# Transposes of a hybrid decoder layer on TensorE, issued in pairs of groups

## Chip, core and metric

One core of one Trainium2 chip runs the whole kernel. The metric is the device time of one execution in microseconds (us), the median of several executions of the same program.

## What is computed

The kernel is one layer of a decoder trunk on 512 tokens of width 1024, in float32. Three mixers share one input projection, each output is gated, projected, and merged:

```python
h = rmsnorm(x, g_pre[i])
(gq, gk, gv, ga, gz, dq, dk, dv, iq, ik, iw, dz, xq, xz, gates) = split_cols(h @ w_in[i])
y_gla = gla_mixer(gq, gk, gv, ga, gz, w_gla_a_up[i], b_gla_a[i], g_gla[i])   # chunked linear attention, 4 heads
y_dsa = dsa_mixer(dq, dk, dv, iq, ik, iw, dz, rel_bias)                      # top-k attention, 8 heads, 2 kv heads
y_mem = cross_mixer(xq, xz, rmsnorm(mem, g_mem[i]), w_mem_kv[i])             # 256 memory tokens, 4 heads
s_gla, s_dsa, s_mem = jnp.split(jax.nn.sigmoid(gates), N_BRANCH, axis=-1)
merged = (s_gla * (y_gla @ w_gla_out[i]) + s_dsa * (y_dsa @ w_dsa_out[i]) + s_mem * (y_mem @ w_x_out[i]))
x = x + rmsnorm(merged @ w_o[i], g_post[i])
```

Each mixer ends in a product that contracts over keys or chunks, so its probabilities (or its normalised output) have to be transposed first. TensorE does that, 128x128 at a time, against an identity matrix.

## The kernel before

Every float32 product is made of three faster ones: each operand is split into a high part (ScalarE, `high`, L94) and the rest (VectorE, `low`, L98 and L100), and `mm3` (L107 to L109) adds high by high, high by low and low by high in one PSUM bank. The weights come in 1 MB loads on SyncE's queue and are split the same way (`whi`, `wlo`).

The program is a list of units, one per 128 columns of a weight matrix and 512 tokens. A unit has four quarters, and a quarter is six matmuls of 512 columns on TensorE (`unit_t`), or as many of 256 columns (`unit_n`). The order of the rest is written out by hand: `at(name, s, fn)` puts a piece of work behind quarter `s` of a unit (counted on into the following units), and the loop at the end of `trunk` (L1104) emits quarter by quarter what stands there. Pieces with the same slot are emitted in the order in which they were put. The engines then run their own queues in that order and meet by semaphores.

The pieces that matter here:

- `dsa_schedule` (L757) orders one pair of query heads, `hp` 0 to 3. A pair has eight pieces `c`: four blocks of 128 queries, `qb = c // 2`, times two heads. For each `c`, `dsa_bias` (GpSimd) adds position bias and mask, `dsa_probs` makes logits and exponentials, `dsa_norm` divides by the sum (VectorE), `dsa_turn` (L710) transposes the `qb + 1` blocks of probabilities into a PSUM bank `tpp` and takes the high part `pth` (ScalarE), `dsa_low` (L726) takes the low part `ptl` (VectorE), and once per two pieces `dsa_out` (L739) multiplies with the values into the PSUM bank `pov`; its second matmul (L108) is the first to read `ptl`. `step` is the distance between two pieces in quarters: 3 for `hp` 0, 2 for the others.
- `gla_y` (L650) transposes half of a linear attention head's output into a bank `to` (four transposes, L654), multiplies it with gain and gate on VectorE (L657) and splits it. `gla_turn_k` (L593) transposes keys into a bank `tk` (L597), with `kkl` as its low part. `gla_att` ends in the copy `attz` (L587) on VectorE.
- `x_turn` (L877) transposes the probabilities of 256 queries of a memory head into `xtp` (four transposes, L886) and splits them into `xpth` and `xptl`; `x_out` (L891) multiplies with the values into `xpo`.

`tpp`, `to`, `tk` and `xtp` take turns in the two PSUM buffers of the tag `tp` (`PSB`, L70): a bank is free again when both ScalarE and VectorE have read it.

Of the kernel before, what the change touches and what calls it, by code (L numbers as in the profile page):

```python
# [57 lines left out]
def trunk(ctx, tc, x, x_t, mem, w_in, w_c, w_kv, w_out, w_o, cols, g_mem, g_post, w_up, toe, out):  # L58
# [115 lines left out]
    def at(name, s, fn, *a):  # L174
        slots.setdefault(4 * where[name] + s, []).append((fn, a))
# [581 lines left out]
    def dsa_schedule(hp, name, step):  # L757
        def put(s, fn, *a):
            at(name, s, fn, hp, *a)
        put(-3, dsa_start)  # L760
        for c in range(8):
            put(4 + step * c, dsa_norm, c)
        for c in range(8):
            s = 2 + step * c
            put(max(s - 2, 1), dsa_bias, c)
            put(s, dsa_probs, c)
            put(s + 5, dsa_turn, c)
            put(s + 7, dsa_low, c)
            if c % 2:
                put(s + 9, dsa_out, c // 2)  # L770

    win_t("dk", dk_done)
# [222 lines left out]
    for h in range(4):  # L995
        z = f"gz{h}"
        if h < 2:
            at(z + ".0", h, gla_att, h, 0)
            at(z + ".0", h + 1, gla_att, h, 1)
            at(z + ".0", h + 2, gla_turn_k, h)  # L1000
            for p in range(3):
                at(z + ".1", 2*p + h, gla_state, h, p)
            after = 6 + h
        else:
            v = f"gv{h}"
            at(v + ".1", 0, gla_att, h, 0)
            at(v + ".1", 1, gla_att, h, 1)
            at(v + ".1", 2, gla_turn_k, h)
            for p in range(3):
                at(z + ".0", 2+p, gla_state, h, p)  # L1010
            after = 2
        for i in range(2):
            at(z + ".1", after + 2 * i, gla_out, h, i)
            at(z + ".1", after + 2 * i + 1, gla_norm, h, i)
            at(z + ".1", after + 10 + 2 * i, gla_y, h, i)
    for i in range(16):
        at("gz1.0", 2 + 6 * i, topk_max)
        at("gz1.0", 5 + 6 * i, topk_drop)
    at("gz1.0", 2 + 6 * 16, topk_mask)
    dsa_schedule(0, "gate02.0", 3)  # L1020
    for i in range(2):
        at("dq1.0", i, dsa_end, 0, i)
    for hp in range(1, 4):
        dsa_schedule(hp, f"dz{hp}.1", 2)
        for i in range(2):
            at(f"dz{hp}.1", 26 + i, dsa_end, hp, i)
# [5 lines left out]
    for h in range(4):  # L1032
        n = f"mv{h}.0"
        for i in range(2):
            for j in range(2):
                at(n, 1 + 4 * i + 2 * j, x_logits, h, i, j)
        at(n, 5, x_norm, h, 0)
        at(n, 9, x_norm, h, 1)
        at(n, 9, x_turn, h, 0)
        at(n, 11, x_turn, h, 1)  # L1040
        at(n, 13 if h == 0 else 17, x_out, h, 0)
        at(n, 15 if h == 0 else 19, x_out, h, 1)
# [8 lines left out]
    with tc.manual_schedule():  # L1051
# [7 lines left out]
        for k in range(4):  # L1059
            h, c = k // 2, slice(512 * (k % 2), 512 * (k % 2) + 512)  # L1060
# [114 lines left out]
def build(arrays):  # L1175
    import concourse.bacc as bacc
    nc = bacc.Bacc("TRN2", target_bir_lowering=False, num_devices=1, dynamic_dma_scratch_size=1024)
    aps = [nc.dram_tensor(n, v.shape, mybir.dt.from_np(v.dtype), kind="ExternalInput").ap()
           for n, v in arrays.items()]
    out = nc.dram_tensor("out", (T, D), F32, kind="ExternalOutput").ap()  # L1180
    with tile.TileContext(nc) as tc:
        trunk(tc, *aps, out)
    return nc
# [8 lines left out]
```

## Time and profile before

| | us |
|---|---|
| median of 3 runs | 834.88 (834.76 to 835.01) |
| the profiled execution, its own time | 834.8 |
| its span, first to last instruction | 833.1 |
| TensorE busy within the span | 818.7 |
| VectorE busy | 473.6 |
| ScalarE busy | 337.6 |
| GpSimd busy | 50.4 |

The sums below are made against the profiled execution, 834.8 us, of which 1.7 us lie outside the span; it stands 0.08 us under the median. In the views, PE is TensorE's matmul and PEld its weight load, DVE is VectorE, ACT is ScalarE, POOL is GpSimd. Matmuls are pipelined: the time that one takes of the stream is read from start to start, not from its duration.

### The profile page before, as it was taken

The numbers are of one execution on the slowest core, as the hardware profiler recorded it, in microseconds if no ns is written. First come the engines' busy times: TensorE is split into PE (matmuls) and PEld (weight loads), VectorE is DVE, ScalarE is ACT, GpSimd is POOL, SyncE is SP. The second block draws the span as 40 slices with busy tenths as digits, with TensorE's granted clock in tenths as the row PEclk, the third lists the DMA queues.
The fourth block names the chain that finished last, engine by engine and source line by source line (L and its number), as shares of the span: only waits on it lengthen the run. The fifth ranks groups of instructions, "written<-read, shape, count | busy, mean of one in ns | idle before, by whom it ended". The sixth has DMA issues, their size and how long they took to land.

```text
span 833.1 us, 10783 instructions
## 1 busy us (share of the span) xinstructions
PE 818.7 (98%) x4320; PEld 703.9 (84%) x4320; DVE 473.6 (57%) x850; ACT 337.6 (41%) x608; POOL 50.4 (6%) x74
## 2 busy tenths in 40 slices
PE   8989999999999999999999999999999999999997
PEld 7988888989888888888888888889989898888885
DVE  4759677888686435446676543545655554343623
ACT  6587554453423223334444422334434343322320
POOL 1000010010000030032131000000000000000000
PEclk9999999999999999999999999999999999999999
DMA  9324121121222231232131124322324142226402
GB/s 327 122 102 138 51 96 57 52 101 55 98 101 101 101 109 69 101 108 95 51 112 66 51 101 176 101 101 101 114 90 148 55 152 72 83 98 225 154 1 102
DMA packets 16387, 86.30 MB, mean 104 GB/s; under 512 B 2064, under 2 KB 2576, under 8 KB 7760
## 3 DMA queue, kind: packets, MB, share of 16 engines
q1 hardware_dynamic: 15472, 84.29, 28.4%
q10 hardware_dynamic: 864, 1.32, 0.4%
q8 instruction: 34, 0.56, 0.3%
q14 instruction: 17, 0.14, 0.0%
HBM read 82.42 MB, written 2.10 MB: 101 GB/s over the span
## 4 chain that ended last, share of the span: by engine, by line
PE 86%; ACT 5%; DVE 5%; DMA 3%; issue 2%; SPq 0%; DVEq 0%; POOLq 0%; POOL 0%; ACTq 0%
PE out L109 5%; PE out L108 5%; PE out L107 5%; PE pfin L109 2%; PE pfin L108 2%; PE pfin L107 2%; DMA wraw<-w_in 1%; DMA x<-x 1%; DVE wlo L98 1%; ACT whi L94 1%; PE tpp L721 1%; PE pov L108 1%; PE pov L109 1%; PE lg L108 1%; PE lg L109 1%
## 5 line engine op out<-in xcount | busy, mean ns | idle before, releaser
L98 DVE TENSOR_TENSOR wlo<-wraw,whi 128x1024 fp32r<-128x1024 f32 (+1 forms) x135 | 163.4, 1211 | 84.3 <-ACT whi L94 83.5
L94 ACT ACTIVATE whi<-wraw 128x1024 fp32r<-128x1024 f32 (+1 forms) x135 | 139.3, 1039 | 22.5 <-PE out L108 19.6
L107 PE MATMUL out<-yh,whi 128*128 128x512 f32 x192 | 75.3, 392 | 0.0
L109 PE MATMUL out<-yh,wlo 128*128 128x512 f32 x192 | 74.8, 390 | 0.0
L108 PE MATMUL out<-yl,whi 128*128 128x512 f32 x192 | 74.8, 389 | 0.0
L707 ACT ACTIVATE bm<-bm,nm 128x128 f32<-128x128 f32 (+3 forms) x32 | 18.0, 564 | 73.6 <-DVE nm L705 71.8
L691 POOL TENSOR_TENSOR bm<-toe,madd 128x128 f32<-128x128 f32 (+3 forms) x32 | 31.2, 993 | 194.4 <-DVE wlo L98 134.3
L109 PEld LDWEIGHTS out<-yh,wlo 128*128 128x128 f32 x192 | 36.0, 188 | 7.5
L107 PEld LDWEIGHTS out<-yh,whi 128*128 128x128 f32 x192 | 36.1, 188 | 7.3
L108 PEld LDWEIGHTS out<-yl,whi 128*128 128x128 f32 x192 | 36.1, 188 | 7.2
L94 ACT ACTIVATE yh<-th 128x512 fp32r<-128x512 f32 x16 | 10.1, 632 | 44.0 <-DVE th L657 24.9
L512 DVE SCALAR_TENSOR_TENSOR gth<-gth,out 128x512 f32<-128x512 f32 x16 | 11.0, 687 | 28.0 <-PE out L109 28.0
L273 POOL TENSOR_TENSOR rstd<-var,mhalf 128x1 f32<-128x1 f32 x6 | 3.3, 552 | 374.9 <-DVE var L952 289.7
L470 DVE MATCH_REPLACE8 madd<-m,madd 128x256 f32<-128x256 f32 (+2 forms) x48 | 25.6, 543 | 0.0
L466 DVE MAX8 m<-madd 128x8 f32<-128x256 f32 (+2 forms) x48 | 23.6, 547 | 0.0
L705 DVE CUSTOM_DVE_ANT_0 bm<-lg,bm 128x128 f32<-128x128 f32 (+3 forms) x32 | 15.5, 485 | 13.0 <-PE lg L109 7.6
L751 DVE TENSOR_TENSOR ydsa<-pov,th 128x128 f32<-128x128 f32 x32 | 7.8, 286 | 22.5 <-PE pov L109 22.1
L94 ACT ACTIVATE pth<-tpp 128x128 fp32r<-128x128 f32 (+3 forms) x32 | 13.7, 429 | 13.4 <-PE tpp L721 13.4
L456 DVE SCALAR_TENSOR_TENSOR madd<-relu,iw,madd 128x256 f32<-128x256 f32 (+2 forms) x21 | 12.9, 616 | 9.2 <-ACT relu L452 8.9
L949 ACT ACTIVATE sq<-pfin 128x512 f32<-128x512 f32 x8 | 4.8, 598 | 31.6 <-PE pfin L109 31.6
L98 DVE TENSOR_TENSOR yl<-th,yh 128x512 fp32r<-128x512 f32 x16 | 11.1, 692 | 11.2 <-ACT yh L94 11.2
L98 DVE TENSOR_TENSOR ptl<-tpp,pth 128x128 fp32r<-128x128 f32 (+3 forms) x32 | 15.4, 482 | 0.0
(1024 smaller groups left out, 2357.0 us busy)
## 6 DMA issues: line engine op xcount, KB each, us to landing
wraw<-w_in SPq DMA_DIRECT2D x43, 1024.0 KB, 4.8
wraw<-w_out SPq DMA_DIRECT2D x12, 1024.0 KB, 4.8
wraw<-w_kv SPq DMA_DIRECT2D x8, 1024.0 KB, 4.7
wraw<-w_o SPq DMA_DIRECT2D x4, 1024.0 KB, 4.8
x<-x SPq DMA_DIRECT2D x4, 512.0 KB, 9.1
toe<-toe SPq DMA_DIRECT2D x8, 256.0 KB, 5.2
xres<-x SPq DMA_DIRECT2D x4, 512.0 KB, 8.5
xt<-x_t SPq DMA_DIRECT2D x3, 512.0 KB, 7.8
```

Source lines behind the costliest of these rows:

```text
L94: act.activation(hi, src, AF.Copy, scale=scale)
L98: dve.tensor_tensor(lo, src, f(hi), op=OP.subtract)
L107: pe.matmul(o, lh, rh, start=first, stop=False)
L108: pe.matmul(o, lh, rl, start=False, stop=False)
L109: pe.matmul(o, ll, rh, start=False, stop=last)
L456: dve.scalar_tensor_tensor(sc, r[:, :n], iw[:, b, h:h + 1], sc, op0=OP.mult, op1=OP.add)
L466: dve.max(out=M8[b], in_=maskadd[b])
L470: dve.match_replace(out=maskadd[b], in_to_replace=M8[b], in_values=maskadd[b], imm_value=-FMAX)
L512: dve.scalar_tensor_tensor(th, th, 1.0, p, op0=OP.add, op1=OP.mult)
L691: pool.tensor_tensor(bm[:, :n], Q[hp]["toe"][i][:, 384 - 128 * qb:512], maskadd[qb], op=OP.add)
L705: dve.tensor_tensor_reduce(out=bm[:, :n], in0=lg[:, :n], in1=bm[:, :n], scale=-1.0, scalar=FMAX, op0=OP.add, op1=OP.min, accum_out=nm)
L707: act.activation(bm[:, :n], bm[:, :n], AF.Exp, scale=-1.0, bias=nm, accum_out=su)
```

## The change

Transposes that stood one group per head or half are put side by side: both pieces of one block of queries (`c - 1` and `c`) in the slot of the second, both halves of `gla_y` in one slot, both halves of `x_turn` in one slot. The low parts `dsa_low` of both pieces stand together too. Nothing is added or left out, and the slots of `dsa_out`, of the norms and of `x_out` stay.

```diff
             put(max(s - 2, 1), dsa_bias, c)
             put(s, dsa_probs, c)
-            put(s + 5, dsa_turn, c)
-            put(s + 7, dsa_low, c)
             if c % 2:
+                for d in (c - 1, c):
+                    put(s + 5, dsa_turn, d)
+                for d in (c - 1, c):
+                    put(s + 7, dsa_low, d)
                 put(s + 9, dsa_out, c // 2)
...
             at(z + ".1", after + 2 * i + 1, gla_norm, h, i)
-            at(z + ".1", after + 10 + 2 * i, gla_y, h, i)
+            at(z + ".1", after + 12, gla_y, h, i)
...
         at(n, 9, x_norm, h, 1)
-        at(n, 9, x_turn, h, 0)
+        at(n, 11, x_turn, h, 0)
         at(n, 11, x_turn, h, 1)
```

TensorE's queue in the last head pair (`hp` 3), around the `dsa_out` of its first block of queries (`pov`, which reads the pieces `c` 0 and 1), a piece of the difference; the other blocks of `hp` 1 to 3 read alike:

```order
-L721 MATMUL tpp<-ident,bm 128x128 x2
...
 L107 MATMUL pov<-pth,dvh 128x256
 L108 MATMUL pov<-ptl,dvh 128x256
 L109 MATMUL pov<-pth,dvl 128x256
-L721 MATMUL tpp<-ident,bm 128x128 x2
...
+L721 MATMUL tpp<-ident,bm 128x128 x4
```

Before, the transposes of the next even piece (`c` 2) stood ahead of `pov` and those of the odd piece (`c` 3) right behind it; now all four stand behind it, so `pov` comes earlier in TensorE's order by the transposes of the even piece.

VectorE's queue in head pair 2, second block of queries (`c` 2 and 3), before:

```order
L751 TENSOR_TENSOR ydsa<-pov,th 128x128 x2
L98 TENSOR_TENSOR ptl<-tpp,pth 128x2x128
L98 TENSOR_TENSOR wlo<-wraw,whi 128x1024
L736 RECIPROCAL rc<-su 128x1
L737 TENSOR_SCALAR bm<-bm,rc 128x384
L705 ISA bm,nm<-lg,bm 128x512
L705 ISA nm 128x1
L490 SCALAR_TENSOR_TENSOR th<-th,dz3.0_4001 128x512
L98 TENSOR_TENSOR ptl<-tpp,pth 128x2x128
```

and now:

```order
L751 TENSOR_TENSOR ydsa<-pov,th 128x128 x2
L98 TENSOR_TENSOR wlo<-wraw,whi 128x1024
L736 RECIPROCAL rc<-su 128x1
L737 TENSOR_SCALAR bm<-bm,rc 128x384
L705 ISA bm,nm<-lg,bm 128x512
L705 ISA nm 128x1
L490 SCALAR_TENSOR_TENSOR th<-th,dz3.0_3995 128x512
L98 TENSOR_TENSOR ptl<-tpp,pth 128x2x128 x2
```

The even piece's low part moved from ahead of the weight split `wlo` to directly ahead of the odd piece's, behind the gate `th` (L490).

VectorE's queue at the linear attention head 1, whose `gla_y` stands beside the keys' transposes of head 2 (a piece of the difference):

```order
-L657 SCALAR_TENSOR_TENSOR th<-to,col,th 128x512
-L98 TENSOR_TENSOR yl_1720<-th,yh_1719 128x512
 L587 COPY_PREDICATED attz<-cmask,pa 128x512
 L98 TENSOR_TENSOR al<-attz,ah 128x512
...
 L98 TENSOR_TENSOR kkl<-tk,kkh 128x384
 L98 TENSOR_TENSOR vl<-gv2.1_1672,vh 128x512
+L657 SCALAR_TENSOR_TENSOR th<-to,col,th 128x512
+L98 TENSOR_TENSOR yl_1764<-th,yh_1763 128x512
 L657 SCALAR_TENSOR_TENSOR th<-to,col,th 128x512
 L98 TENSOR_TENSOR yl_1774<-th,yh_1773 128x512
```

The first half's two instructions went from ahead of `attz` to behind `kkl`; on TensorE both `to` groups now follow `tk`, so the second one takes the bank that `tk` holds until `kkl` has read it.

## Rows read from the trace of the kernel before

**Rows 1.** The page: busy time of TensorE, and shares of the chain that ended last.
```profile
PE 818.7 (98%) x4320; PEld 703.9 (84%) x4320; DVE 473.6 (57%) x850; ACT 337.6 (41%) x608; POOL 50.4 (6%) x74
...
PE 86%; ACT 5%; DVE 5%; DMA 3%; issue 2%; SPq 0%; DVEq 0%; POOLq 0%; POOL 0%; ACTq 0%
```

**Rows 2.** Timeline of TensorE: start us, duration us, engine, line, operation. Eight transposes; four.
```profile
532.11 0.39 PE L109 MATMUL out<-yh,wlo 128*128 128x512 f32 x1
532.34 1.03 PE L294 MATMUL xps<-ident,xn 128*128 128x128 f32 x8
533.13 0.48 PE L107 MATMUL out<-yh,whi 128*128 128x512 f32 x1
533.44 0.40 PE L108 MATMUL out<-yl,whi 128*128 128x512 f32 x1
...
575.51 0.39 PE L109 MATMUL xq1.0_5296<-hh,wlo 128*128 128x512 f32 x1
...
576.41 0.40 PE L108 MATMUL xq1.0_5296<-hl,whi 128*128 128x512 f32 x1
```

**Rows 3.** Timeline: odd piece's low part, then the load of its reader; hp 1 to 3.
```profile
404.86 0.55 DVE L98 TENSOR_TENSOR ptl<-tpp,pth 128x384 fp32r<-128x384 f32 x1
406.22 0.19 PEld L108 LDWEIGHTS pov<-ptl,dvh 128*128 128x128 f32 x1
...
429.37 0.42 DVE L98 TENSOR_TENSOR ptl<-tpp,pth 128x256 fp32r<-128x256 f32 x1
430.23 0.19 PEld L108 LDWEIGHTS pov<-ptl,dvh 128*128 128x128 f32 x1
...
454.40 0.28 DVE L98 TENSOR_TENSOR ptl<-tpp,pth 128x128 fp32r<-128x128 f32 x1
454.74 0.19 PEld L108 LDWEIGHTS pov<-ptl,dvh 128*128 128x128 f32 x1 [0.57 <-DVE ptl L98]
...
461.87 0.42 DVE L98 TENSOR_TENSOR ptl<-tpp,pth 128x256 fp32r<-128x256 f32 x1
462.50 0.19 PEld L108 LDWEIGHTS pov<-ptl,dvh 128*128 128x128 f32 x1
```

**Rows 4.** Timeline of VectorE, head pair 2, between the low parts of c 2 and 3.
```profile
424.69 1.23 DVE L98 TENSOR_TENSOR wlo<-wraw,whi 128x1024 fp32r<-128x1024 f32 x1 [0.85 <-ACT whi L94]
...
428.77 0.69 DVE L490 SCALAR_TENSOR_TENSOR th<-th,dz3.0_4001 128x512 f32<-128x512 f32 x1 [1.43 <-ACT th L489]
```

**Rows 5.** Timeline of TensorE and VectorE at the linear attention head 1.
```profile
161.53 0.60 PE L654 MATMUL to<-ident,on 128*128 128x128 f32 x4
162.51 0.45 PE L583 MATMUL pa<-qd,kte 128*64 128x64 f32 x4
...
164.23 0.73 DVE L587 COPY_PREDICATED attz<-cmask,pa 128x512 f32<-128x512 uint8 x1
...
166.17 0.60 PE L654 MATMUL to<-ident,on 128*128 128x128 f32 x4
...
167.40 0.55 DVE L98 TENSOR_TENSOR kkl<-tk,kkh 128x384 fp32r<-128x384 f32 x1
```

**Rows 6.** Timeline of VectorE and GpSimd: the same two lines, without and with GpSimd.
```profile
416.35 1.21 DVE L98 TENSOR_TENSOR wlo<-wraw,whi 128x1024 fp32r<-128x1024 f32 x1
417.48 0.69 DVE L98 TENSOR_TENSOR yl<-ydsa,yh 128x512 fp32r<-128x512 f32 x1
...
448.11 2.34 POOL L691 TENSOR_TENSOR bm<-toe,madd 128x512 f32<-128x512 f32 x1 [3.86 <-DVE ydsa L751]
...
449.22 1.78 DVE L98 TENSOR_TENSOR yl<-ydsa,yh 128x512 fp32r<-128x512 f32 x1
```

**Rows 7.** Stretch of the eight transposes: us, then busy us (x) by engine, granted clock, DMA.
```profile
531.00:535.00 4.00, 4.00 (x23) 3.43 (x22) 2.24 (x5) 2.03 (x3) 0.00 (x0) 1.00 0.00 0
```

**Rows 8.** Timeline, first memory head: low part of the second half, first value matmul.
```profile
580.40 0.68 DVE L98 TENSOR_TENSOR xptl<-xtp,xpth 128x512 fp32r<-128x512 f32 x1
...
582.14 0.39 PE L107 MATMUL xpo<-xpth,mvh 128*128 128x512 f32 x1
```

## The prediction

> **What bounds the kernel now.** I read the page first: TensorE is busy 98% of the span, and 86% of the chain that ended last is its own work [rows 1]. So what counts is the time that its stream of matmuls takes from start to start, and any wait in it. Next the timeline of TensorE around two sizes of transpose group, to price a group from start to start [rows 2]. Then, since the change makes others wait differently, how much time lies between the instruction that TensorE waits for and the place where it is wanted: for the attention's low parts [rows 3], what VectorE waits for between them [rows 4], the linear attention's bank [rows 5] and the memory attention's low part [rows 8]. Last, two disturbances: GpSimd beside VectorE [rows 6], and the granted clock [rows 7].
>
> **What a merge gives.** The change turns 48 groups of transposes into 24: 32 of the top-k attention with one to four transposes each (80 in all), 8 of four for the gated outputs, 8 of four for the memory attention. No transpose is removed, so only what a group costs besides its transposes can be gained. One step of the stream, a matmul of 512 columns, is 532.34 - 532.11 = 0.23 us [rows 2]. From the last matmul ahead of a group to the second behind it are two steps and the group: with eight transposes 533.44 - 532.11 = 1.33, less 0.46 is 0.87 us; with four (one call of x_turn lies between the two rows) 576.41 - 575.51 = 0.90, less 0.46 is 0.44 us. A transpose is then (0.87 - 0.44) / 4 = 0.1075 us, and a group's own cost 0.44 - 0.43 = 0.01 us. So 24 merges give 24 x 0.01 = **0.24 us**. The rows are rounded to 0.01, so a merge lies between 0 and 0.02 us: 0 to 0.5 us.
>
> A rule speaks against longer groups. In the rows the granted clock over the stretch with eight transposes in a row is 1.00, so 2.4 GHz [rows 7], and a row of eight costs no more per transpose than one of four. By the Trainium skill ("TensorE: Matmul & The Clock Gate", Part 4: PE-mode transpose) a transpose doesn't count as busy TensorE in the way a matmul does; by that a longer group would be a risk for the clock, and here it would cost time instead of 0.24 us gained. I go by the row; the rule is a rival below.
>
> **What the attention's value product waits for.** In head pairs 1 to 3 (step 2) two things change at each pov. First, TensorE reaches it earlier: the next even piece's transposes now stand behind it. By 0.01 + 0.1075 each that is 0.12, 0.23, 0.33 and 0.44 us for one to four. Reaching it earlier gains nothing by itself, but if the low part isn't there, that much becomes a wait. Second, VectorE now makes the even low part directly ahead of the odd one. Does it finish the odd one later by it? Only if the place that the even one left isn't used. In pair 2 it isn't: behind the old place VectorE waits 0.85 us for ScalarE's weight split, then 1.43 us for ScalarE's tanh [rows 4]; both follow from exponentials and not from the even low part. So the odd one ends later by the even one's place in the queue: its length less the 0.08 us by which VectorE overlaps successive instructions (416.35 + 1.21 - 417.48 [rows 6]), 0.42 - 0.08 = 0.34 us for c 2 and 0.55 - 0.08 = 0.47 us for c 4 [rows 3]. At c 0 the odd low part is on a chain that the even one held up, so nothing is added.
>
> The spare time is from the low part's end to the start of the weight load that reads it, less 0.06 us, the distance when TensorE was really waiting (454.40 + 0.28 to 454.74) [rows 3]. The four closest places:
> - pair 1, c 5: 404.86 + 0.55 to 406.22, less 0.06: 0.75 us; needed 0.44 + 0.47 = 0.91; wait 0.16.
> - pair 2, c 3: 429.37 + 0.42 to 430.23, less 0.06: 0.38 us; needed 0.33 + 0.34 = 0.67; wait 0.29.
> - pair 3, c 1: none, TensorE's load already waits 0.57 us [rows 3]; 0.23 more.
> - pair 3, c 3: 461.87 + 0.42 to 462.50, less 0.06: 0.15 us; needed 0.67; wait 0.52, which holds the 0.23 of c 1, because a TensorE that is late already finds its data at the next place.
>
> Sum 0.16 + 0.29 + 0.52 = **0.97 us lost**. The trace of before shows no such wait for a doubled low part, hence both ends. At least: VectorE uses the free place after all, and only the earlier arrival counts, 0.23 in pair 3 and nothing elsewhere. At most: no lateness carries over (0.16 + 0.29 + 0.23 + 0.52 = 1.20) and the c 0 low part of pair 3 adds its 0.20: 1.40 us. Pair 0 has step 3, with pov and the next transposes a quarter or more apart; I cost it at nothing.
>
> The banks: the next pair of transposes needs both tp buffers free, but stands right behind the pov that has already waited for both low parts, so nothing is added there.
>
> **The linear attention.** In heads 0, 2 and 3 the first half's four transposes move two quarters later, into the banks that were free before. In head 1 they move behind the keys' transposes, and the second half now wants their bank, which kkl frees. Before, kkl ended at 167.40 + 0.55 = 167.95 [rows 5], long behind. But now attz isn't queued behind the first half's product: it can start when pa ends, 162.51 + 0.45 = 162.96, less the group of 0.44 that went from ahead of it, 162.52 instead of 164.23. That is 1.71 us earlier, and with it the chain to kkl: 166.24, and with 0.06 for the semaphore 166.30. TensorE wants the second half's first weights at 166.17 - 0.44 + 0.43 = 166.16, loaded one place (0.1) ahead, 166.06. Wait **0.24 us**; 0 if the chain shrinks a bit more, 0.5 if VectorE gains only the 1.43 us that two such instructions take (0.74, as long as attz, and 0.69).
>
> **The memory attention.** Both low parts of a head now come together. For head 0 the second ended at 581.08 and was wanted at 582.14 [rows 8]: 1.06 us. Another 0.60 (0.68 less 0.08) ahead of it leaves 0.46; heads 1 to 3 put x_out four quarters later. Nothing.
>
> **Sum.** -0.24 + 0.97 + 0.24 = +0.97 us on the profiled 834.80: 835.77, so **835.8 us** (the median of the runs stands 0.08 higher). The bounds: -0.5 + 0.23 + 0 gives 834.5; 0 + 1.4 + 0.5 gives 836.7. A measurement of this kernel can tell about 0.2%, 1.7 us, from no change, so this is the same time.
>
> **Rivals.**
> 1. *The step back to ordinary matmuls is the cost.* The first matmul behind a group takes 533.44 - 533.13 = 0.31 instead of 0.23 us [rows 2]. If that belongs to the group, 24 merges save 24 x 0.08 = 1.9 us, and if nothing waits the time is 834.88 - 1.92, about 832.9. For it: each group shows it. Against it: eight transposes cost 0.87, two fours 0.88, so the last transpose hides what the next matmul shows. Chance 0.04.
> 2. *Slower: GpSimd's adds fall on the tight places.* In pair 3 an add of GpSimd takes 2.34 us, and VectorE's instruction beside it 1.78 us where the same line took 0.69 in pair 2 [rows 6]: one held up the other, 1.09 us. Many adds start when the transposes free a buffer, and these move by two quarters. By the Trainium skill ("SBUF — State Buffer", Who interferes with whom) a VectorE instruction with two inputs in SBUF and a GpSimd one that reads SBUF fully block each other, whichever comes second; rows 6 agree. It decides when an add falls between the low parts of a pair with under 0.4 us to spare (pair 2 c 3, pair 3): one gives 835.8 + 1.1 = 836.9, two 838.0. Against it: the place in before already has one, in the tightest pair, and if that one goes the wait at 454 us goes with it, some 0.3 us. Chance 0.09.
> 3. *The clock falls in long groups.* A group has 144 / 24 = 6 transposes, 0.65 us; at the lower of the two levels, 1.2 GHz, each would take twice that, 24 x 0.65 = 15.6 us more, 850. Against it stands 1.00 in the stretch with eight [rows 7]. Chance 0.01.
>
> That the change doesn't do what it says is excluded: the order shows the groups of two, four, six and eight.
>
> **How the numbers follow.** My case has 0.85, rival 1 0.04, rivals 2 and 3 0.10; 0.01 is left for a gain that I don't see. Within 0.2% is my case; faster 0.05, slower 0.10. The range starts at 834.2 (the lower bound, and the wait in pair 3 gone as well) and ends at 837.0, which takes in the upper bound and one collision.
>
> **What would show it.** Right: transposes 0.11 us apart through merged groups and 0.01 us less per merge; TensorE waiting for ptl in pair 2 (c 3) and pair 3 (c 1 and 3), together near 1 us; one wait of 0.1 to 0.4 us ahead of the second half's transposes of head 1 for VectorE. Wrong in the first term: a merged group of eight well under 0.87 us. Wrong in the second: no wait for ptl beyond the one of before, or one in every pair. Any clock below 1.00 in these stretches makes it rival 3; stretched VectorE rows beside GpSimd's adds ahead of a late ptl make it rival 2.

## The result, and the profile after

The changed kernel takes **840.06 us** (median of 4 runs, 839.02 to 841.0) against 834.82 us for the kernel before (4 runs, 834.5 to 835.01): a ratio of 1.0059, 95% interval 1.0047 to 1.0071. It is slower, by more than the 0.2% that can be told, and 3 us above the top of the predicted range.

The profiled execution took 841.0 us with a span of 839.3, 6.2 us more than the span before. To see where, take the same matmul in both timelines of TensorE and subtract the starts; the difference, called the offset below, grows where time is lost. The tiles are weight units in the order of the program; the number counts a tile's L107 matmuls.

| TensorE reaches | before | after | offset | since the mark above |
|---|---|---|---|---|
| `pc`, 4th (start-up over) | 25.91 | 27.20 | 1.29 | 1.29 |
| `dq0.0`, 7th (linear attention over) | 237.25 | 240.08 | 2.83 | +1.54 |
| `gate10.0`, 5th (top-k attention over) | 470.92 | 477.36 | 6.44 | +3.61 |
| `xz3.1`, 1st (memory attention over) | 688.03 | 694.22 | 6.19 | -0.25 |

The first 1.29 us lie ahead of every changed instruction: the executions of most kernels here, before's among them, lie on two levels some 1.5 us apart, and two of the change's four, the profiled one included, are on the upper. The changed stages make 1.54 + 3.61 - 0.25 = 4.9 us, about what the other two executions show (839.02 and 839.41 against some 834.4).

The page after: busy time, and the chain that ended last.

```profile
PE 820.4 (98%) x4320; PEld 705.2 (84%) x4320; DVE 476.7 (57%) x850; ACT 336.9 (40%) x608; POOL 51.2 (6%) x74
...
PE 77%; DVE 11%; ACT 7%; issue 3%; DMA 2%; SPq 0%; DVEq 0%; POOLq 0%; POOL 0%; ACTq 0%
```

Against [rows 1] TensorE's share of the chain has fallen from 86% to 77%, VectorE's risen from 5% to 11%: TensorE waits more, and for VectorE. VectorE itself is 3.1 us busier (476.7 against 473.6) with the same 850 instructions, so some of them took longer. The view of TensorE's waits (engine, line, waited for: total us, times, longest) has two in the changed stages that before hardly had; the third line is before's only one for `ptl`, and before has none at `gv2.0`:

```profile
PE pov L108 <- DVE ptl L98: 3.0, 3, 1.4
PE gv2.0_1615 L108 <- DVE wlo L98: 1.1, 1, 1.1
...
PE pov L108 <- DVE ptl L98: 0.2, 1, 0.2
```

**The merged group.** The timeline of TensorE around the first memory head's transposes, now eight in a row, answers to [rows 2], and the last line is the stretch with the granted clock as in [rows 7].

```profile
584.70 0.39 PE L109 MATMUL xq1.0_5296<-hh,wlo 128*128 128x512 f32 x1
584.93 1.03 PE L888 MATMUL xtp<-ident,xe 128*128 128x128 f32 x8
585.72 0.48 PE L107 MATMUL xq1.1_5349<-hh,whi 128*128 128x512 f32 x1
586.03 0.40 PE L108 MATMUL xq1.1_5349<-hl,whi 128*128 128x512 f32 x1
...
581.00:586.00 5.00, 5.00 (x28) 4.24 (x27) 2.25 (x5) 2.26 (x5) 0.00 (x0) 1.00 0.44 184
```

586.03 - 584.70 is 1.33 us, as for the eight in [rows 2], and there is no loss of clock, which is 1.00 in this stretch (rival 3).

**The low parts.** Timeline of VectorE and of the weight loads, the same four places as in [rows 3]: the pair of low parts (x2), then the load of the first reader, with its wait.

```profile
407.62 1.01 DVE L98 TENSOR_TENSOR ptl<-tpp,pth 128x384 fp32r<-128x384 f32 x2
408.69 0.19 PEld L108 LDWEIGHTS pov<-ptl,dvh 128*128 128x128 f32 x1 [0.38 <-DVE ptl L98]
...
434.12 0.75 DVE L98 TENSOR_TENSOR ptl<-tpp,pth 128x256 fp32r<-128x256 f32 x2
434.92 0.19 PEld L108 LDWEIGHTS pov<-ptl,dvh 128*128 128x128 f32 x1 [0.64 <-DVE ptl L98]
...
460.22 0.48 DVE L98 TENSOR_TENSOR ptl<-tpp,pth 128x128 fp32r<-128x128 f32 x2
460.75 0.19 PEld L108 LDWEIGHTS pov<-ptl,dvh 128*128 128x128 f32 x1 [1.62 <-DVE ptl L98]
...
467.89 0.75 DVE L98 TENSOR_TENSOR ptl<-tpp,pth 128x256 fp32r<-128x256 f32 x2
468.69 0.19 PEld L108 LDWEIGHTS pov<-ptl,dvh 128*128 128x128 f32 x1 [0.36 <-DVE ptl L98]
```

All four wait, as predicted. But the third is far longer than the rest, and a fifth place that the prediction did not have waits just as long: pair 2, c 1 (the load at 426.70 waits 1.69 us). A sixth, pair 2, c 5, waits 0.34 us at 442.79. The timeline around it, VectorE (DVE) with GpSimd (POOL) and ScalarE (ACT), answers to [rows 6], and in its second half to [rows 4]:

```profile
418.62 3.53 POOL L691 TENSOR_TENSOR bm<-toe,madd 128x512 f32<-128x512 f32 x2 [14.60 <-PE tpp L721]
...
418.94 2.07 DVE L98 TENSOR_TENSOR wlo<-wraw,whi 128x1024 fp32r<-128x1024 f32 x1
420.93 1.77 DVE L98 TENSOR_TENSOR yl<-ydsa,yh 128x512 fp32r<-128x512 f32 x1
...
423.73 0.62 ACT L707 ACTIVATE bm<-bm,nm 128x384 f32<-128x384 f32 x1 [3.98 <-DVE nm L705]
...
424.35 0.58 ACT L94 ACTIVATE dqh<-dq3.1_3899 128x512 fp32r<-128x512 f32 x1
...
424.96 0.69 DVE L100 SCALAR_TENSOR_TENSOR dql<-dq3.1_3899,dqh 128x512 fp32r<-128x512 f32 x1 [1.32 <-ACT dqh L94]
425.57 0.68 DVE L98 TENSOR_TENSOR yl<-ydsa,yh 128x512 fp32r<-128x512 f32 x1
426.17 0.48 DVE L98 TENSOR_TENSOR ptl<-tpp,pth 128x128 fp32r<-128x128 f32 x2
...
426.70 0.39 PE L108 MATMUL pov<-ptl,dvh 128*128 128x256 f32 x1 [1.36 <-DVE ptl L98]
```

GpSimd's two adds of 512 columns are released together, by transposes that have read `bm` (`<-PE tpp`), and run back to back over 3.53 us (1.30 and 2.15 us, with 0.08 between). Beside them VectorE's `wlo` takes 2.07 instead of 1.21 us and `yl` 1.77 instead of 0.69 [rows 6]: 1.94 us of VectorE gone. VectorE passes the delay on: the exponential (L707) waits 3.98 us for the score step that VectorE makes behind `yl`, ScalarE's `dqh` stands behind the exponential, and VectorE idles 1.32 us for `dqh` with the low parts two instructions behind. Before, these two adds started 8 us apart. Timeline of the kernel before:

```profile
411.22 1.30 POOL L691 TENSOR_TENSOR bm<-toe,madd 128x512 f32<-128x512 f32 x1 [10.41 <-PE tpp L721]
...
419.41 1.29 POOL L691 TENSOR_TENSOR bm<-toe,madd 128x512 f32<-128x512 f32 x1 [6.89 <-PE tpp L721]
...
420.42 0.69 DVE L100 SCALAR_TENSOR_TENSOR dql<-dq3.1_3904,dqh 128x512 fp32r<-128x512 f32 x1 [1.32 <-ACT dqh L94]
```

The second ran for 1.29 us partly beside VectorE's idle 1.32 us, and stretched nothing there. Pair 3 after the change repeats pair 2: adds of 3.53 us at 452.74, `wlo` 2.13 at 452.99, `yl` 1.78 at 455.04, low parts at 460.22. The adds reach the smaller waits too: two of 384 columns run back to back from 402.03, and the `wlo` beside them, ahead of the low parts of pair 1, c 4 and 5, takes 1.82 us.

**Linear attention.** Head 1's group with the wait of its second bank, answering to [rows 5] (timeline of VectorE and of the weight loads):

```profile
165.22 0.74 DVE L587 COPY_PREDICATED attz<-cmask,pa 128x512 f32<-128x512 uint8 x1 [1.39 <-PE pa L583]
...
168.41 0.55 DVE L98 TENSOR_TENSOR kkl<-tk,kkh 128x384 fp32r<-128x384 f32 x1
...
169.02 0.42 PEld L654 LDWEIGHTS to<-ident,on 128*128 128x128 f32 x4 [0.24 <-DVE kkl L98]
```

That is the 0.24 us predicted. The rest of this stage's loss follows head 0's group, where nothing was expected. Timeline of VectorE, and TensorE's matmul that waits:

```profile
138.08 0.42 DVE L98 TENSOR_TENSOR Sh<-S,Sh 128x256 fp32r<-128x256 f32 x1 [2.29 <-ACT Sh L94]
...
142.58 0.69 DVE L98 TENSOR_TENSOR yl<-th,yh 128x512 fp32r<-128x512 f32 x1 [0.70 <-ACT yh L94]
...
144.63 0.69 DVE L98 TENSOR_TENSOR yl<-th,yh 128x512 fp32r<-128x512 f32 x1 [0.70 <-ACT yh L94]
...
154.75 1.22 DVE L98 TENSOR_TENSOR wlo<-wraw,whi 128x1024 fp32r<-128x1024 f32 x1
...
156.02 0.39 PE L108 MATMUL gv2.0_1615<-wlo,hh 128*128 128x256 f32 x1 [1.06 <-DVE wlo L98]
```

And from the kernel before, the same instructions of VectorE and TensorE:

```profile
137.43 0.43 DVE L98 TENSOR_TENSOR Sh<-S,Sh 128x256 fp32r<-128x256 f32 x1 [0.97 <-ACT Sh L94]
...
152.05 1.22 DVE L98 TENSOR_TENSOR wlo<-wraw,whi 128x1024 fp32r<-128x1024 f32 x1
...
153.44 0.28 PE L108 MATMUL gv2.0_1615<-wlo,hh 128*128 128x256 f32 x1
```

Before, the first half's gating product and split stood ahead of `Sh` and used a time in which VectorE would otherwise have idled: now it idles 2.29 us there instead of 0.97, and does both halves afterwards, each with its own 0.70 us of waiting for ScalarE. Ten microseconds later `wlo` is 2.70 us behind its place before. 1.37 of that is TensorE's own offset there; the other 1.33 are too much, since `wlo` ended at 153.27 for a matmul at 153.44.

**Memory attention.** Timeline, answering to [rows 8]:

```profile
586.37 1.28 DVE L98 TENSOR_TENSOR xptl<-xtp,xpth 128x512 fp32r<-128x512 f32 x2
...
588.54 0.39 PE L107 MATMUL xpo<-xpth,mvh 128*128 128x512 f32 x1
```

The low parts are there at 587.65, 0.89 us ahead: nothing waits, as predicted.

### The profile page after: what moved, and what is told of

It is laid out like the page before. It is cut to its first block, busy times and chain, and to the rows that moved or that the text cites. A ratio compares the mean times of both kernels' runs of the same rounds, so it can differ in the third digit from the quotient of the medians.

```text
span 839.3 us, 10788 instructions
## 1 busy us (share of the span) xinstructions
PE 820.4 (98%) x4320; PEld 705.2 (84%) x4320; DVE 476.7 (57%) x850; ACT 336.9 (40%) x608; POOL 51.2 (6%) x74
## 3 DMA queue, kind: packets, MB, share of 16 engines
q10 hardware_dynamic: 864, 1.32, 0.4%
## 4 chain that ended last, share of the span: by engine, by line
PE 77%; DVE 11%; ACT 7%; issue 3%; DMA 2%; SPq 0%; DVEq 0%; POOLq 0%; POOL 0%; ACTq 0%
PE out L108 5%; PE out L109 5%; PE out L107 5%; DVE wlo L98 3%; ACT whi L94 2%; PE pfin L109 2%; PE pfin L108 2%; PE pfin L107 2%; DMA x<-x 1%; DMA wraw<-w_in 1%; PE tpp L721 1%; DVE bm L705 1%; DVE yl L98 1%; ACT bm L707 1%; PE pov L108 1%
## 5 line engine op out<-in xcount | busy, mean ns | idle before, releaser
L98 DVE TENSOR_TENSOR wlo<-wraw,whi 128x1024 fp32r<-128x1024 f32 (+1 forms) x135 | 165.9, 1229 | 91.3 <-ACT whi L94 90.1
L107 PE MATMUL out<-yh,whi 128*128 128x512 f32 x192 | 75.0, 391 | 0.0
L707 ACT ACTIVATE bm<-bm,nm 128x128 f32<-128x128 f32 (+3 forms) x32 | 18.1, 566 | 80.2 <-DVE nm L705 80.2
L107 PEld LDWEIGHTS out<-yh,whi 128*128 128x128 f32 x192 | 36.1, 188 | 7.3
L94 ACT ACTIVATE pth<-tpp 128x128 fp32r<-128x128 f32 (+3 forms) x32 | 12.0, 426 | 11.1 <-PE tpp L721 11.1
L108 PE MATMUL pov<-ptl,dvh 128*128 128x256 f32 x40 | 11.9, 298 | 3.1 <-DVE ptl L98 3.0
```

Of the source, the lines that this page charges most:

```text
L94: act.activation(hi, src, AF.Copy, scale=scale)
L98: dve.tensor_tensor(lo, src, f(hi), op=OP.subtract)
L107: pe.matmul(o, lh, rh, start=first, stop=False)
L108: pe.matmul(o, lh, rl, start=False, stop=False)
L707: act.activation(bm[:, :n], bm[:, :n], AF.Exp, scale=-1.0, bias=nm, accum_out=su)
```

## The experiments

Intervals are of the ratio to the kernel before on the same chip.

**Which part costs.** Three kernels each carry one part of the change alone.

`x_only`:
```diff
-        at(n, 9, x_turn, h, 0)
+        at(n, 11, x_turn, h, 0)
```


> Only the memory attention's transposes of a head go in one group of eight; everything else as before. My theory (a group's own cost is all there is to gain, nothing waits): four merges, about 0.06 to 0.3 us in that stage, so the time of before within 0.3 us, and the stage's offset falls by under 0.1 us per head. Rival (a cost of long groups shows in the whole program): the same slowdown per group as the full change would need, 5.2 us / 24 merges x 4 = 0.9 us slower.

`gla_only`:
```diff
-            at(z + ".1", after + 10 + 2 * i, gla_y, h, i)
+            at(z + ".1", after + 12, gla_y, h, i)
```


> Only the gated outputs' transposes of the linear attention go two at a time. Theory: head 0 loses 1.3 us because both split blocks of VectorE run back to back behind ScalarE and gv2.0's matmul comes before its VectorE weight split wlo is done (a wait of about 1.1 us there), head 1 loses 0.2 us for the bank: 1.3 to 1.5 us slower than before. Rival (the wait at gv2.0 is scatter of this one profile, as the 1.3 us at the start is): 0.2 us, and gv2.0 doesn't wait.

`dsa_only`:
```diff
-            put(s + 5, dsa_turn, c)
-            put(s + 7, dsa_low, c)
             if c % 2:
+                for d in (c - 1, c):
+                    put(s + 5, dsa_turn, d)
+                for d in (c - 1, c):
+                    put(s + 7, dsa_low, d)
```


> Only the top-k attention's transposes go two pieces at a time. Theory (two collisions of GpSimd's adds with VectorE, in pairs 2 and 3, on top of the waits that I predicted): 3.4 to 3.8 us slower than before, waits for ptl at pair 2 c 1 and pair 3 c 1 of some 1.4 us each. Rival (the predicted term alone, the doubled low part): 1.0 us slower, waits of 0.2 to 0.5 us.

| kernel | median us | before | ratio | change of the offset in its stage (minus is faster) |
|---|---|---|---|---|
| `x_only` | 834.16 | 834.46 | 1.0000 (0.9991 to 1.0009) | -0.28 |
| `gla_only` | 835.95 | 834.46 | 1.0020 (1.0011 to 1.0029) | +1.41 |
| `dsa_only` | 838.09 | 834.46 | 1.0047 (1.0035 to 1.0060) | +3.66 |

The parts add up: -0.28 + 1.41 + 3.66 = 4.8 us against 4.9 together. The waits of 1.1 us at `gv2.0` and of 1.36 and 1.29 us at `pov` are in these profiles too, so they are not scatter of one execution. The memory attention's merged groups gain by the offset (`x_only`), though less than the times can tell.

**Are GpSimd's adds the cause in the top-k attention?** Two kernels leave the adds of pairs 1 to 3 out, one with the transposes as before and one with the full change.

`noadd_before`, `noadd_after`:
```diff
+        if hp == 0:
-        pool.tensor_tensor(bm[:, :n], Q[hp]["toe"][i][:, 384 - 128 * qb:512], maskadd[qb], op=OP.add)
+            pool.tensor_tensor(bm[:, :n], Q[hp]["toe"][i][:, 384 - 128 * qb:512], maskadd[qb], op=OP.add)
...
-        dve.tensor_tensor_reduce(out=bm[:, :n], in0=lg[:, :n], in1=bm[:, :n], scale=-1.0,
+        dve.tensor_tensor_reduce(out=bm[:, :n], in0=lg[:, :n], in1=(maskadd[qb] if hp else bm)[:, :n], scale=-1.0,
```


> The kernel before, without GpSimd's bias adds for head pairs 1 to 3 (the position bias is left out there; VectorE's score step reads the mask table instead). It is the base for the next run. Theory (GpSimd and VectorE hold each other up): VectorE's second score step in pair 3 no longer takes 1.78 us, and TensorE's one wait for ptl of 0.57 us goes: 0.3 to 1 us faster than before. Rival (the adds hold up nothing): the same time as before and the wait of 0.57 us stays.

> The same omission in the full change. Theory (the two long waits in pairs 2 and 3 are GpSimd's adds, back to back, holding VectorE up): both long waits for ptl shrink to under 0.5 us, VectorE's wlo and yl in pair 2 take 1.2 and 0.7 us instead of 2.07 and 1.77, and the attention's loss against the run without adds in the old order falls from 3.8 us to about 1 us (the term that I predicted), so some 2.5 us in all with the linear attention's 1.5. Rival (the order of the low parts is enough by itself, the adds only happen beside it): the long waits stay at over 1 us, and the loss stays at 3.4 us or more, 5 in all.

Measured: 834.08 us in the old order (0.9996, 0.9987 to 1.0005) and 835.59 in the new (1.0010, 1.0001 to 1.0020; before 834.53). The timeline of VectorE in `noadd_after`, at the place in pair 2 shown above:

```profile
418.58 1.23 DVE L98 TENSOR_TENSOR wlo<-wraw,whi 128x1024 fp32r<-128x1024 f32 x1
419.73 0.68 DVE L98 TENSOR_TENSOR yl<-ydsa,yh 128x512 fp32r<-128x512 f32 x1
...
423.87 0.48 DVE L98 TENSOR_TENSOR ptl<-tpp,pth 128x128 fp32r<-128x128 f32 x2
```

Same order, normal lengths, and no wait of TensorE for `ptl` is left in the list; one weight load, of pair 2, c 5, still waits 0.24 us. Over the top-k attention the offset falls by 0.79 us in the new order and by 0.53 in the old (there only the old wait at 454 us goes): without the adds the merged order is 0.26 us *better*, with them 3.61 worse. This went beyond the theory, which still expected its own 1 us of waits here. The whole loss of this stage hangs on the adds. Leaving them out also frees the score steps from waiting for them, but that wait was not there: in the change the second add of pair 2 ended at 422.15, and the first score step of 512 columns, which reads such a sum, began at 431.40. (The expectation of `noadd_before` calls the line of 1.78 us a score step; it is the `yl` of [rows 6].)

**Or could the low parts simply stand elsewhere?** `low6`, the full change with both low parts one place earlier:
```diff
-                    put(s + 7, dsa_low, d)
+                    put(s + 6, dsa_low, d)
```


> The full change, but VectorE makes both low parts of a pair one place earlier in its order (put at s+6 instead of s+7). If the low parts come late because of their place in VectorE's order (the predicted mechanism, the doubled low part), the waits for ptl shrink by the work that now stands behind them, and the attention loses under 1.5 us instead of 3.8: 2 us or more faster than the full change. If they are late because GpSimd's adds hold VectorE up ahead of them, the two long waits stay at 1 us or more and the time stays within 1 us of the full change's 840.1.

836.0 us (1.0017, 1.0008 to 1.0025), 4 us below the full change's median; the offsets put 3.46 us of that in the top-k attention. Timeline of VectorE in pair 2, and of TensorE in pair 3:

```profile
417.12 2.13 DVE L98 TENSOR_TENSOR wlo<-wraw,whi 128x1024 fp32r<-128x1024 f32 x1
419.17 1.78 DVE L98 TENSOR_TENSOR yl<-ydsa,yh 128x512 fp32r<-128x512 f32 x1
...
421.33 0.48 DVE L98 TENSOR_TENSOR ptl<-tpp,pth 128x128 fp32r<-128x128 f32 x2
...
470.59 0.39 PE L108 MATMUL pov<-ptl,dvh 128*128 128x256 f32 x1 [0.67 <-DVE ptl L98]
```

My two alternatives were not a clean pair, and the result is both: VectorE is held up as before (2.13, 1.78), yet the low parts start 0.4 us behind it (421.33 against 420.95) instead of 3.5, because they no longer stand behind the wait for `dqh`. In pair 2 the collision is needed for the loss, and so is the place that lets it reach TensorE. Pair 3 does not test this as well: its adds ran free there (2.55 us for both at 448.71), and only `wlo` was stretched (2.15 us at 450.19), not `yl`. Of the stage's 3.61 us 0.15 are left, and the wait of 0.67 us, a new one for c 5 of pair 3, costs more than that; the rest is a gain, the old wait at 454 us among it.

**Is the double wait for ScalarE the cause in the linear attention?** `gla_inter`, the full change with the two halves interleaved:
```diff
-        y = zs[f"gz{h}", i]
-        dve.scalar_tensor_tensor(y, to, ggla[:, i:i + 1], y, op0=OP.mult, op1=OP.mult)
-        y_split(2 * h + i, y)
+            y = zs[f"gz{h}", i]
+            dve.scalar_tensor_tensor(y, to, ggla[:, i:i + 1], y, op0=OP.mult, op1=OP.mult)
+            ys.append(y)
+        for i in range(2):
+            k = 2 * h + i
+            yh[k], yl[k] = k2("yh", f"yh{k}", F32R), k2("yl", f"yl{k}", F32R)
+            high(yh[k], ys[i])
+        for i in range(2):
+            k = 2 * h + i
+            low(yl[k], ys[i], yh[k])
```


> The full change, but in the linear attention both halves' gating products come first, then both high parts, then both low parts, so that VectorE waits for ScalarE's high part once and not twice. Theory (the two waits of 0.70 us for ScalarE and the late start push gv2.0's wlo back): the wait of 1.06 us at gv2.0 falls to 0.4 us or less, and the time by 0.7 to 1.3 us against the full change, 839 or a little under. Rival (wlo is late because of the merged group's later place alone): the wait stays at 1 us.

838.02 us (1.0044, 1.0031 to 1.0058), and the wait at `gv2.0` is gone altogether; the stage's offset grows by 0.16 instead of 1.54 us, near the 0.24 us of head 1's bank. Timeline of VectorE:

```profile
139.18 1.40 DVE L661 SCALAR_TENSOR_TENSOR th<-to,col,th 128x512 f32<-128x512 f32 x2
140.62 1.35 DVE L98 TENSOR_TENSOR yl<-th,yh 128x512 fp32r<-128x512 f32 x2
```

(Line 661 is L657 of the change.) The same four instructions take 139.18 to 141.97, 2.8 us, where they took 141.13 to 145.32, 4.2 us. So the late start alone doesn't make `wlo` late. Nor do two waits alone: the kernel before has both (0.70 us each, ahead of 135.76 and 141.93), the first of them ahead of `Sh`. It took the two together.

**Versions that might beat before.** `mix_lowfirst` keeps the linear attention as before and the other two parts merged, with the low parts ahead of the normalizations of their place:
```diff
+        for c in range(8):
+            put(8 + step * (c | 1), dsa_low, c)
         for c in range(8):
             put(4 + step * c, dsa_norm, c)
...
-                for d in (c - 1, c):
-                    put(s + 7, dsa_low, d)
```


> A version from what was found: memory attention and top-k attention merged, the linear attention as before, and VectorE makes both low parts of a pair right ahead of the normalizations that share their place. Theory (the low parts' place in VectorE's order decides, and 20 merges give about 0.015 us each): no wait for ptl above 0.2 us, the last wait of low6 (0.67 us) and the 0.57 us of before gone, 0.8 to 1.6 us faster than before, 833.0 to 833.7. Rival (VectorE's normalizations come late in their turn and hold up the exponentials): a new wait takes the place, and it is no faster than before.

833.93 against 834.53 us, 0.9994 (0.9986 to 1.0003), less than the 0.8 to 1.6 us expected, and no difference that the times can tell: the offset falls by 0.35 us in the top-k attention and 0.26 in the memory attention. A wait of 0.28 us is left in pair 3, c 5, where the low parts stand behind a weight split of VectorE, which itself waits 1.43 us for ScalarE. Does any of the 0.35 come from the merged groups? `early_only` leaves every transpose where it was:
```diff
+        for c in range(8):
+            put(8 + step * c, dsa_low, c)
         for c in range(8):
             put(4 + step * c, dsa_norm, c)
...
-            put(s + 7, dsa_low, c)
```


> The kernel before with every transpose where it was, and VectorE's low parts one place earlier, ahead of the normalization that shares the place. If the gain of the version before this one comes from the low parts' place, the wait of 0.57 us in pair 3 c 1 goes here too and the time is 0.3 to 0.6 us below before; if it comes from the merged groups, the time stays within 0.2 us of before's.

834.11 against 834.67 us, 0.9991 (0.9982 to 1.0000), and the stage gains 0.53 us, all of it at one place, the wait of 0.57 us in pair 3 [rows 3]. So merging gives nothing there, taken together, that moving the low part doesn't give alone. Place by place it does: up to 447 us, with 13 merges done, `mix_lowfirst`'s offset has fallen by 0.30 us (0.02 each) where `early_only`'s stays, and the new wait at c 5 then costs 0.52.

Two attempts failed on something else. `best` is `mix_lowfirst` with c 4 and 5 of pair 3 unmerged:
```diff
-            put(8 + step * (c | 1), dsa_low, c)
+            put(8 + step * (c if (hp, c) == (3, 4) else c | 1), dsa_low, c)
...
-                    put(s + 5, dsa_turn, d)
+                    put(s + 5 - (step if (hp, d) == (3, 4) else 0), dsa_turn, d)
```


> The version of mix_lowfirst, with pieces 4 and 5 of pair 3 not merged, since the merged one waits there for ScalarE's high part. Theory: its last wait for ptl (0.3 us) goes, and the time is 0.5 to 0.9 us below mix_lowfirst's offset in that stage's end, 833.0 to 833.6. Rival (the collision of the adds then falls there): no faster than mix_lowfirst.

`lowpair_only` has the transposes of before and pairs only the low parts:
```diff
-            put(s + 7, dsa_low, c)
             if c % 2:
+                for d in (c - 1, c):
+                    put(s + 7, dsa_low, d)
```


> The kernel before with the top-k attention's transposes where they were, and only VectorE's two low parts of a pair made together at the later place. Theory (the paired transposes free two score buffers at once, so that GpSimd's adds come back to back beside VectorE; the paired low parts alone do little): no VectorE instruction of pair 2 is stretched beyond the one pair of before, the odd low parts come 0.34 to 0.47 us later, and all but pair 3 c 3 (0.15 us to spare) have the room: 0 to 0.4 us slower than before. Rival (the low parts' later place is the cost, the adds are not): waits for ptl of over 1 us, 2.5 us or more slower than before.

`best` took 835.75 (1.0017, 1.0008 to 1.0026), `lowpair_only` 866.4 us (1.0372, 1.0353 to 1.0391), against 833.0 to 833.6 and at most 0.4 us of loss expected. TensorE's waits, of the first and then of the second:

```profile
PE tpp L721 <- DVE ptl L98: 1.9, 1, 1.9
```

```profile
PE tpp L721 <- DVE ptl L98: 25.8, 11, 3.8
...
390.48 0.41 PE L721 MATMUL tpp<-ident,bm 128*128 128x128 f32 x2 [2.40 <-DVE ptl L98]
```

In the first I had also taken the wrong cause for the wait of `mix_lowfirst`: not ScalarE's high part but the weight split ahead, as said above. And I had forgotten the two `tpp` banks in both. A low part that waits for its partner keeps its bank, and the next transposes, which now want it, stand in front of TensorE. `lowpair_only` therefore says nothing about whether paired low parts cost anything by themselves; it shows that with two banks low parts can't be paired where the transposes aren't. Two of its waits, the 2.40 us above and 3.77 us at 476, were each followed by some 3.4 us in which the granted clock was 0.50, the lower level of 1.2 GHz (391.1 to 394.4 and 476.4 to 479.7), which adds to the loss.

The two parts that lost nothing, together, are `early_x`: the diffs of `early_only` and `x_only`.

> The two parts that lost nothing, together: VectorE's low parts one place earlier with every transpose of the top-k attention where it was, and the memory attention's transposes in groups of eight. Theory (both gains are separate places of TensorE's stream and add): the wait of 0.57 us in pair 3 c 1 gone (0.52 us) and 0.07 us per head of the memory attention (0.28 us), 0.8 us below before in the offsets, 0.4 to 1.2 us in the medians. Rival (one of the two was scatter): 0.5 us or less.

833.87 against 834.58 us, 0.9993 (0.9984 to 1.0002). The trace has both gains, 0.53 us at the one place in pair 3 and 0.28 in the memory attention, and no wait for `ptl` in its list; the medians differ by 0.7 us, but the interval takes in no change at all, so the gain rests on the offsets of one profile each.

## Why the prediction was wrong

The prediction was 835.8 us and the result 840.06. Two steps failed: what stands ahead of the low parts on VectorE was taken as unchanged (0.97 us predicted for this stage's waits, 3.61 us lost in it), and the linear attention's heads 0, 2 and 3 were put at nothing (1.3 us lost behind head 0).

**What a merge gives: right in kind, too small.** Twenty-four merges were to give 0.24 us. By the offsets the four of the memory attention give 0.28 (`x_only`), 0.07 each, and the sixteen of the top-k attention 0.26 by `noadd_after` against `noadd_before`, which holds a new stall of 0.18 us in pair 2: 0.44, or 0.03 each. That is three to seven times the predicted 0.01 us, and still small. Eight transposes still take 0.87 us up to the second matmul behind them; the prediction's window ended there, and 0.05 of the 0.07 us lie behind it. Before, the ten matmuls from the second behind the first group of four took 2.32 us (576.41 to 578.73), those behind a group of eight in `x_only` 2.27 (579.09 to 581.36). Why the matmuls behind a group differ stays open. Rival 1 had the size nearly right for the memory attention (0.08 us per merge), but not for the top-k attention, and the 0.31 us it pointed at is still there (586.03 - 585.72). Rival 3 falls: the stretch above with eight in a row, and the linear attention's at 168 us, show a granted clock of 1.00. What the Trainium skill says ("TensorE: Matmul & The Clock Gate", Part 4: PE-mode transpose), that a transpose doesn't count as busy TensorE in the way a matmul does, cost nothing here.

**The wait for `ptl`: the step that failed.** "In pair 2 it isn't: behind the old place VectorE waits ..." treated all that VectorE does ahead of the low parts as unchanged. The waits that it forecast are at their places, but by what they cost the stream in `dsa_only`, beyond `low6`, two of them are twice as long (pair 1, c 5: 0.16 predicted, 0.33; pair 2, c 3: 0.29 and 0.56), and in `noadd_after`, with the same order and the same doubled low parts, none of the four is left. So neither the large waits nor these are made by the doubled low part and TensorE's earlier arrival alone. I followed what the transposes hand on, and not what they hand back: with the transposes of two pieces in one place two `bm` buffers come free at once, and GpSimd refills them back to back exactly where VectorE has two long instructions. That was rival 2, mechanism and place (pairs 2 and 3), given 0.09. Its condition, an add "between the low parts", was too narrow: the adds fell ahead of both, on `wlo` and `yl`, and the delay came through ScalarE. With two collisions it gave 838.0, and with the 1.3 us of head 0 that is 839.3, near the 839.02 and 839.41 us measured. That closeness is partly luck: a collision took 1.94 us of VectorE and not 1.1, and the 0.97 us under it does not come without the adds. The argument against it, that the place in before already had one, was no argument: the old one stayed out of everybody's way but once, the new ones come twice, with two adds each.

By the Trainium skill ("SBUF — State Buffer", Who interferes with whom) of a VectorE instruction with two inputs in SBUF and a GpSimd one that reads SBUF, the one that comes second is blocked until the first is done. The trace fits that: the first add ran from 418.62 to 419.92, as long as one alone; `wlo`, begun at 418.94, needs 1.21 us and ended at 421.01; the second add, begun at 420.00, ended at 422.15, and `yl`, begun at 420.93, at 422.70. They took turns.

**Linear attention.** The term for head 1 was right (0.24 predicted; 0.24 idle). "In heads 0, 2 and 3 the first half's four transposes move two quarters later, into the banks that were free before" was true, but counted only the banks. VectorE's product and split move with the transposes, out of a time in which it idled, and a weight split behind them had 0.17 us to spare: 1.3 us. Heads 2 and 3 lost nothing.

**Memory attention.** Right: no wait, with 0.89 us to spare where 0.46 was predicted.

## What to carry to other kernels

A group moved on one engine moves the release of every buffer that it reads: ask what refills them, on which engine, and what that runs beside, before pricing the group itself. Work that goes with a moved instruction on an in-order engine may have been sitting in idle time; look for the next thing behind it that has little to spare, however far. And where a loss arrives through a queue, moving the small product that is waited for to the earliest place its inputs allow may take it away while the disturbance stays, as `low6` did in pair 2.

## What the runs showed that was not expected

- A short wait cost TensorE's stream more than the idle time that the view shows. In `dsa_only` the wait of 1.36 us in pair 2 moves the offset by 1.84 where `low6`, without it, has 0.21: 1.63 us. That of 0.30 at c 3 of that pair moves it by 0.89 instead of 0.33: 0.56. The difference is some 0.26 in both. Most of it is how idle time is counted, from the end of a pipelined matmul: the one ahead (256 columns) is shown with 0.28 us, but takes 0.12 of the stream. The rest is that the first matmul after the wait takes 0.22 us to the next start instead of 0.12.
- The start differs between profiles. The stretch of 20 to 30 us (busy us by engine, granted clock, DMA) after, and then before:

```profile
20.00:30.00 10.00, 8.16 (x34) 6.50 (x33) 5.09 (x6) 5.74 (x8) 1.04 (x1) 0.83 0.42 152
```

```profile
20.00:30.00 10.00, 9.47 (x57) 8.09 (x56) 6.36 (x8) 6.16 (x8) 1.04 (x1) 1.00 0.47 159
```

  In the profile after, TensorE waited until 21.72 for `whi` (1.31 us) and until 22.98 for `wlo` (0.53 us); then its granted clock was 0.50 from 23.1 to 26.4 us, the lower level of 1.2 GHz, and matmuls of 512 columns stood 0.43 us apart instead of 0.23. `dsa_only` and `noadd_after` show the same 0.83 and start 1.25 and 1.21 us late by the offset; `x_only`, which waited 1.22 and 0.53 us there too, kept 1.00. Why only some do stays open.
- Not tried: adds that start apart while transposes stay paired and low parts stay where the change has them.
